# Attention's values in two matmuls a key tile instead of three, softmax sums on GpSimd, and three score banks for four

## The chip, the cores and the metric

The kernel runs on one core of one Trainium2 chip. The core has TensorE (PE, with its weight loads as PEld), VectorE (DVE), ScalarE (ACT), GpSimd (POOL) and SyncE (SP), which run their own instruction streams in order and wait for each other on semaphores. The metric is the device time of one execution in microseconds (µs), the median of three runs.

## The reference

One layer of a bidirectional hybrid encoder is applied to 2048 prompt tokens and 256 sample tokens (2304 together, 18 tiles of 128), in FP32:

```
n = rmsnorm(x);  p = n @ w_in            # 1024 -> 4*512 + 32 + 512 + 2*128
m = mlstm_mixer(...)                     # 8 heads, both directions, chunkwise
s = q . k * 64**-0.5;  P = softmax(s);  o = P @ v      # 8 query heads, 2 key/value heads, d = 64
x = x + concat(m, o) @ w_out
u = dwconv3(rmsnorm(x) @ w_up);  a, g = split(u);  y = rmsnorm(x + (silu(g) * a) @ w_down)
```

Attention is within a request: a prompt query sees the 16 prompt key tiles, a sample query the 2 sample key tiles. The scores are large (the norm weights of q and k carry a factor of 8), so that the softmax is taken with the row maximum subtracted.

## The kernel before

Matmuls run in FP32R, one pass a matmul. To keep FP32 precision an operand is split into a rounded high part and a low remainder, and a product is the sum of three matmuls (high·high, high·low, low·high) in one PSUM bank. The PSUM memory has eight banks; each holds 128 rows of 512 FP32 numbers.

The program has four stages. First the projections of attention's q, k, v and of the gates. Then attention and the mLSTM together: both are Python generators that emit their steps, and a planner (`run_both`) takes a step of the one that is behind, by costs that are written out (`A_PAIR`, `A_MAX`, `A_PREP` for attention, the numbers yielded by `mlstm`); a scheduler then reorders what was emitted by readiness and priority on each engine. After the mLSTM the output projection (`phase_c`, tile `po`) is emitted between attention's steps, and there PE keeps the order in which it was written. Last comes the feed-forward stage, more than half of the time, which the change does not touch.

Attention is worked in 36 blocks of 512 query columns, numbered 0 to 35 here in the order in which they run. Blocks 0, 1, 26 and 27 are the small ones (sample queries, 2 key tiles); the other 32 have 16 key tiles, worked in 8 pairs. Its steps in a large block:

- `prep`: four transposes of q (tile `pq`), copied by ACT.
- `maxstep`, 16 times: one matmul of 512 columns (tile `px`), then a row maximum on DVE (tile `mx`, L570). They are done one block ahead, while the scores of the block before run.
- `scores`, per key tile: two matmuls (L595, L596) into tile `ps`; ACT writes the exponential twice, rounded to `ph` (L599) and in FP32 back into `ps` (L600); DVE writes the remainder `pl = ps - ph` (L601).
- `values`, per key tile, two pairs behind the scores: three matmuls of 512 columns into the one bank `pv` (L613): [v high | ones] with `ph`, v low with `ph`, and [v high | ones] with `pl`. Rows 0 to 63 of `pv` gather the output, rows 64 to 127 the softmax sum, spread over 64 rows by the columns of ones.
- `fin1`: ACT copies both halves of `pv` out. `fin2`, four times: a reciprocal on DVE (L630). `fin3`: POOL multiplies (L634) and stores.

The tiles `pq`, `px`, `ps` and `pr` (the maxima, spread by a matmul) take turns in `SCB` = 4 banks of tag `sc`, one after the other in the order in which they are emitted; `pv` has one bank, and the mLSTM (or the output projection) has three.

The mLSTM works on four head pairs. For each there are the projections (PE, tiles `mj` and `mv`, 256 columns a matmul) and then 18 chunks of output, 72 in all, each with small FP32 matmuls (tiles `mS`, `mI`, `mN`, `mT`), some eight DVE operations on tiles `dm`, `s`, `dn` and `hh`, and on POOL a power (`mr`, L101), two selects on `dm` (L864) and the loads of `dm`.

Of the kernel before, what the change touches and what calls it, by code (L numbers as in the profile page):

```python
# [9 lines left out]
F32 = mybir.dt.float32  # L10
F32R = mybir.dt.float32r
AF = mybir.ActivationFunctionType
ALU = mybir.AluOpType
# [4 lines left out]
P = 128  # L18
# [6 lines left out]
HD = 64  # L25
# [4 lines left out]
ACOL = 2048  # L30
MPRI = 2000
STORE = "sync"
SCB = 4
MB = 2
MJ = 1
BLK = 768
# [21 lines left out]
DMB = 6  # L58
KWB = 2
LEAD = 1.3  # L60
A_PAIR = 2.3
A_MAX = 0.23
A_PREP = 1.0
C_MM = 1.43
# [10 lines left out]
PHB = 6  # L75
PLB = 6
# [12 lines left out]
def f32(ap):  # L89
    return ap.bitcast(F32)  # L90
# [382 lines left out]
def attention(g, tc, s1, s2, pp):  # L473


    nc = g.nc
    sp = s1
    hbs = []
    for grp in range(2):
# [4 lines left out]
        else:  # L484
# [2 lines left out]
                     for hh in (h0, h0 + 2)]  # L487
            hbs += large[0:8] + small + large[8:]
    kv = {}

    def load_kv(grp, k0, k1, after=None):

        if (grp, k0) in kv:
            return
        n = k1 - k0
        sp = s2 if n == NT1 else s1
        kv[(grp, k0)] = parts = []
        for t0 in range(0, n, 4):
            m = min(4, n - t0)
            s = f"{n}_{t0}"  # L500
            kk = sp.tile([P, m * P], F32R, tag="kk" + s, name=f"kk{grp}_{s}", bufs=1)
            kl1 = sp.tile([65, m * P], F32R, tag="kl1" + s, name=f"kl1{grp}_{s}", bufs=1)
            vs = [sp.tile([P, m, P if a == 0 else HD], F32R, tag=f"v{a}" + s, name=f"v{a}{grp}_{s}", bufs=1)
                  for a in range(2)]
            c = slice((k0 + t0) * P, (k0 + t0 + m) * P)
            if after is not None:
                for t in (kk[0:1, 0:1], kk[HD:HD + 1, 0:1], kl1[0:1, 0:1], vs[0][0:1, 0, 0:1], vs[1][0:1, 0, 0:1]):
                    nc.gpsimd.tensor_copy(t, after[0:1, 0:1])
            nc.gpsimd.memset(f32(vs[0][:, :, HD:]), 1.0)
            for r in (0, HD):  # L510
                nc.gpsimd.dma_start(f32(kk[r:r + HD, :]), g.k_d[grp, 0:HD, c])
            nc.gpsimd.dma_start(f32(kl1[0:HD, :]), g.k_d[grp, HD:P, c])
            nc.gpsimd.memset(f32(kl1[64:65, :]), 1.0)
            for a in range(2):
                nc.gpsimd.dma_start(f32(vs[a][:, :, 0:HD]), g.v_d[a, grp, :, k0 + t0:k0 + t0 + m])
            parts.append((kk, kl1, vs))

    class HB:
        pass
# [68 lines left out]
    def scores(s, kp):  # L588
        N = s.N
        parts = []  # L590
        for z in range(2):
            ps = pp.tile([P, 512], F32, tag="sc", name=f"ps{s.nm}_{kp}_{z}")[:, 0:N]
            kk, kl1, _ = s.kv[kp // 2]
# [6 lines left out]
            nc.scalar.activation(ps, ps, AF.Exp)  # L600
            nc.vector.tensor_tensor(pl, ps, f32(ph), ALU.subtract)  # L601
            parts.append((ph, pl))
        return parts

    def values(s, kp, parts):

        N = s.N
        if kp == 0:
            s.pv = pp.tile([P, 512], F32, tag="pv", name="pv" + s.nm, bufs=1)
        vs = [[v[:, (2 * kp + z) % 4, :] for v in s.kv[kp // 2][2]] for z in range(2)]  # L610
        todo = [(vs[z][k], parts[z][0]) for z in range(2) for k in range(2)] + [(vs[z][0], parts[z][1]) for z in range(2)]
        for k, (v, p) in enumerate(todo):
            nc.tensor.matmul(s.pv[0:HD if k in (1, 3) else P, 0:N], v, p, start=(kp == 0 and k == 0),  # L613
                             stop=(2 * kp + 2 == s.nk and k == 5))

    def fin1(s):

        N = s.N
        s.o1 = sp.tile([HD, 512], F32, tag="o1", name="o1" + s.nm, bufs=2)
        s.rs = sp.tile([HD, 512], F32, tag="rs", name="rs" + s.nm, bufs=1)  # L620
        nc.scalar.activation(s.o1[:, 0:N], s.pv[0:HD, 0:N], AF.Copy)
        nc.scalar.activation(s.rs[:, 0:N], s.pv[HD:P, 0:N], AF.Copy)
        s.left = list(range(0, N, P))

    def fin2(s):
# [958 lines left out]
```

## Time and profile before

| | µs |
|---|---|
| runs (3) | 3425.78, 3429.24, 3429.64; median 3429.24 |
| span of the profiled execution, first to last instruction | 3427.2 |
| PE / DVE / ACT / POOL busy | 3329.3 / 2677.3 / 1931.2 / 1120.9 |
| first and last score matmul of attention | 255.7 and 1756 |

The time of the profiled execution as a whole is not listed beside its span; the span lies between the three runs, 2.0 µs under their median, so that what lies around it is small against anything told here.

How to read it: a PE matmul's duration runs from its issue to its modelled end, and the next one starts long before that end; PE's busy share is therefore high even where it is not full, and what a matmul takes from PE is the step from its start to the start of the next. DMA issues, semaphores and register instructions are not counted as busy. "Idle before, releaser" names what ended an engine's wait.

### The profile page before, as it was taken

The numbers are of one execution on the slowest core, as the hardware profiler recorded it, in microseconds if no ns is written. First come the engines' busy times: TensorE is split into PE (matmuls) and PEld (weight loads), VectorE is DVE, ScalarE is ACT, GpSimd is POOL, SyncE is SP. The second block draws the span as 40 slices with busy tenths as digits, with TensorE's granted clock in tenths as the row PEclk, the third lists the DMA queues.
The fourth block names the chain that finished last, engine by engine and source line by source line (L and its number), as shares of the span: only waits on it lengthen the run. The fifth ranks groups of instructions, "written<-read, shape, count | busy, mean of one in ns | idle before, by whom it ended". The sixth has DMA issues, their size and how long they took to land. (4 is left out here: it accounts for less than half of the span.)

```text
span 3427.2 us, 55596 instructions
## 1 busy us (share of the span) xinstructions
PE 3329.3 (97%) x20058; PEld 3098.4 (90%) x20058; DVE 2677.3 (78%) x4654; ACT 1931.2 (56%) x4329; POOL 1120.9 (33%) x1328
## 2 busy tenths in 40 slices
PE   7989999999999999899999999999999999999998
PEld 6878888888888888688899999999999999999998
DVE  6885687777768788967767878789888888888776
ACT  4536666666666767655544444446444446555554
POOL 6653132213232323211244333226233224322222
PEclk9999999999999999999999999999999999999999
DMA  6765342333345444422365232223323213421221
GB/s 220 243 203 159 89 140 86 115 123 98 108 131 160 143 123 139 145 77 94 101 216 198 81 105 87 68 80 133 129 94 103 72 59 128 140 74 62 69 74 50
DMA packets 254756, 404.27 MB, mean 118 GB/s; under 512 B 32112, under 2 KB 156816, under 8 KB 254480
## 3 DMA queue, kind: packets, MB, share of 16 engines
q1 hardware_dynamic: 226576, 358.23, 32.7%
q0 software_dynamic: 11344, 33.04, 3.6%
q10 hardware_dynamic: 16560, 9.44, 0.9%
q8 instruction: 158, 2.59, 0.3%
q14 instruction: 118, 0.97, 0.1%
HBM read 316.73 MB, written 83.90 MB: 117 GB/s over the span
## 5 line engine op out<-in xcount | busy, mean ns | idle before, releaser
L1322 PE MATMUL pd<-act,wd 128*128 128x384 f32 (+1 forms) x3120 | 593.4, 336 | 23.9 <-DVE acc L1324 12.6
L1322 PEld LDWEIGHTS pd<-act,wd 128*128 128x128 f32 x3120 | 539.6, 188 | 32.6 <-DVE acc L1324 18.1
L601 DVE TENSOR_TENSOR pl<-ps,ph 128x512 fp32r<-128x512 f32 x520 | 352.7, 683 | 181.5 <-ACT ps L600 173.4
L1184 PE MATMUL pa<-nt,wut 128*128 128x386 f32 (+2 forms) x2376 | 454.3, 339 | 0.0
L599 ACT ACTIVATE ph<-ps 128x512 fp32r<-128x512 f32 x520 | 309.4, 595 | 243.5 <-PE ps L596 239.5
L1184 PEld LDWEIGHTS pa<-nt,wut 128*128 128x128 f32 x2376 | 421.6, 190 | 0.3 <-ACT u L1200 0.3
L570 DVE TENSOR_REDUCE mx<-px 128x1 f32<-128x512 f32 (+1 forms) x528 | 345.5, 670 | 74.4 <-PE px L569 72.4
L1278 DVE SCALAR_TENSOR_TENSOR y<-u,cw,y 128x768 f32<-128x768 f32 (+1 forms) x264 | 315.6, 1196 | 36.4 <-ACT y L1271 29.3
L1189 POOL TENSOR_TENSOR tw<-ru 128x512 f32<-128x512 f32 x66 | 94.1, 1425 | 732.5 <-DMA ru<-w_up 558.5
L613 PE MATMUL pv<-ph,v 128*128 128x512 f32 (+1 forms) x1040 | 319.4, 401 | 1.0 <-ACT ph L599 0.8
L600 ACT ACTIVATE ps<-ps 128x512 f32<-128x512 f32 x520 | 310.3, 597 | 0.0
L1200 ACT ACTIVATE u<-pa 128x386 f32<-128x386 f32 (+2 forms) x264 | 128.3, 486 | 320.9 <-PE pa L1184 320.7
L1324 DVE TENSOR_TENSOR acc<-pd,acc 128x384 f32<-128x384 f32 (+1 forms) x544 | 280.3, 535 | 35.5 <-PE pd L1322 34.1
L1041 PEld LDWEIGHTS po<-cmx,wo 128*128 128x128 f32 x1728 | 220.7, 191 | 8.2 <-DVE mmx L931 0.6
L1041 PE MATMUL po<-cmx,wo 128*128 128x256 f32 x1728 | 224.2, 284 | 0.4 <-DVE mmx L931 0.4
L595 PE MATMUL ps<-qq,kk 128*128 128x512 f32 x520 | 215.5, 416 | 4.2 <-DVE mx L570 2.4
L569 PE MATMUL px<-kk,qq 128*128 128x512 f32 (+1 forms) x528 | 202.8, 413 | 6.0 <-DVE mx L570 2.9
L596 PE MATMUL ps<-qm,kl 65*128 65x512 f32 x520 | 206.7, 399 | 0.0
L759 PE MATMUL mj<-mn,wm 128*128 128x256 f32 x1296 | 203.0, 289 | 2.8 <-ACT og L773 1.9
L759 PEld LDWEIGHTS mj<-mn,wm 128*128 128x128 f32 x1296 | 187.1, 193 | 19.8 <-ACT og L773 2.0
L769 PEld LDWEIGHTS mv<-wm,mn 128*128 128x128 f32 x1296 | 182.8, 190 | 18.4 <-ACT qb L765 2.5
L769 PE MATMUL mv<-wm,mn 128*128 128x256 f32 x1296 | 196.5, 285 | 1.0 <-ACT qb L765 0.9
(288 smaller groups left out, 7266.6 us busy)
## 6 DMA issues: line engine op xcount, KB each, us to landing
ru<-w_up SPq DMA_DIRECT2D x132, 512.0 KB, 3.4
mn<-n_d SPq DMA_DIRECT2D x216, 256.0 KB, 3.4
rd<-w_down SPq DMA_DIRECT2D x66, 512.0 KB, 3.6
n_d<-n1T SPq DMA_DIRECT2D x18, 1024.0 KB, 5.6
dm<-nm_d POOLq DMA_DIRECT2D x72, 256.0 KB, 4.1
mjn<-n_d SPq DMA_DIRECT2D x72, 256.0 KB, 3.3
mvn<-n_d SPq DMA_DIRECT2D x72, 256.0 KB, 3.1
q_d<-qz SPq DMA_DIRECT2D x18, 512.0 KB, 3.7
```

What stands on the lines that cost most here:

```text
L570: nc.vector.tensor_reduce(s.mx[:, t, z0:z0 + 1], ps[:, 0:w], AX.X, ALU.max)
L599: nc.scalar.activation(ph, ps, AF.Exp)
L600: nc.scalar.activation(ps, ps, AF.Exp)
L601: nc.vector.tensor_tensor(pl, ps, f32(ph), ALU.subtract)
L613: nc.tensor.matmul(s.pv[0:HD if k in (1, 3) else P, 0:N], v, p, start=(kp == 0 and k == 0), stop=(2 * kp + 2 == s.nk and k == 5))
L759: nc.tensor.matmul(pj[:, o], s.w[c][:, a, o * P:(o + 1) * P], nT[c][:, :, h, :], start=(c + o + k == 0), stop=(c == NCC - 1 and k == 2 and ...
L769: nc.tensor.matmul(pv[:, o], nT[c][:, o, a, :], s.w[c][:, h, 256:512], start=(c + o + k == 0), stop=(c == NCC - 1 and k == 2 and o == 1))
L1041: nc.tensor.matmul(po[:, o], wo[z // 2][c][:, a, n], mx[c][:, h, :], start=(c == 0 and k == 0), stop=(c == NCC - 1 and k == 2))
L1184: nc.tensor.matmul(p, w[:, aa, c, :], ops[k][:, c, bb, 0:n], start=c == 0 and i == 0 and not add, stop=c == NCC // 2 - 1 and i == 2, skip_ ...
L1278: nc.vector.scalar_tensor_tensor(y[:, s:e], u[:, s + k:e + k], cw[:, k, jj:jj + 1], y[:, s:e], ALU.mult, ALU.add)
L1322: nc.tensor.matmul(po, wds[j][c // 4][:, aa, c % 4 * P:(c % 4 + 1) * P], acts[j][:, bb, z0:z1], start=(j == 0 and k == 0), stop=(j == len( ...
L1324: nc.vector.tensor_tensor(accs[c][:, z0:z1], po, accs[c][:, z0:z1], ALU.add)
```

## The change

- **Two value matmuls.** The stationary operand of a key tile becomes one tile of 192 columns, [v low | v high | ones]. A matmul with columns 0 to 127 on `ph` writes `pv`: low·`ph` in rows 0 to 63, high·`ph` in rows 64 to 127. A matmul with columns 64 to 191 on `pl` writes a second bank, `pw`: high·`pl` and the sum of `pl`.
- **The sum of `ph`.** In blocks with 16 key tiles POOL adds the first 14 tiles `ph` into `pacc` (13 additions of 128x512), ACT rounds the total to a tile of tag `ph`, POOL writes its remainder to a tile of tag `pl`, and four matmuls with the constant tile `low` ([zeros | ones]) add the rounded total, the remainder and the last two `ph` to rows 64 to 127 of `pw`. Small blocks add their two `ph` by `low` directly.
- **`fin1`** copies rows 64 to 127 of `pv` to `o1` (ACT), adds rows 0 to 63 of `pv` and then of `pw` (two DVE operations of 64x512), and copies the sums out of `pw` (ACT). `o1` has one buffer instead of two.
- **Banks.** `SCB` goes from 4 to 3, and `pw` takes the bank.
- **The planner's cost** of a pair, `A_PAIR`, goes from 2.3 to 1.9.

```diff
-SCB = 4
+SCB = 3
+PSUMS = 14
-A_PAIR = 2.3
+A_PAIR = 1.9
...
+    low = s2.tile([P, P], F32R, name="low1")
+    nc.gpsimd.memset(f32(low[:, 0:HD]), 0.0)
+    nc.gpsimd.memset(f32(low[:, HD:P]), 1.0)
...
-            vs = [sp.tile([P, m, P if a == 0 else HD], F32R, tag=f"v{a}" + s, name=f"v{a}{grp}_{s}", bufs=1)
-                  for a in range(2)]
+            v = sp.tile([P, m, 3 * HD], F32R, tag="v" + s, name=f"v{grp}_{s}", bufs=1)
...
             parts.append((ph, pl))
+            i = 2 * kp + z
+            if s.nk > 2 and i < PSUMS:
+                if i == 1:
+                    s.acc = sp.tile([P, 512], F32, tag="pacc", name="pacc" + s.nm, bufs=1)[:, 0:N]
+                    nc.gpsimd.tensor_tensor(s.acc, f32(s.ph0), f32(ph), ALU.add)
+                elif i:
+                    nc.gpsimd.tensor_tensor(s.acc, s.acc, f32(ph), ALU.add)
+                else:
+                    s.ph0 = ph
+                if i == PSUMS - 1:
+                    s.tot = [sp.tile([P, 512], F32R, tag=t, name=f"{t}{s.nm}_s", bufs=n)[:, 0:N]
+                             for t, n in (("ph", PHB), ("pl", PLB))]
+                    nc.scalar.activation(s.tot[0], s.acc, AF.Copy)
+                    nc.gpsimd.tensor_tensor(s.tot[1], s.acc, f32(s.tot[0]), ALU.subtract)
...
-        todo = [(vs[z][k], parts[z][0]) for z in range(2) for k in range(2)] + [(vs[z][0], parts[z][1]) for z in range(2)]
-        for k, (v, p) in enumerate(todo):
-            nc.tensor.matmul(s.pv[0:HD if k in (1, 3) else P, 0:N], v, p, start=(kp == 0 and k == 0),
-                             stop=(2 * kp + 2 == s.nk and k == 5))
+        sums = list(s.tot) if last and s.nk > 2 else []
+        for z in range(2):
+            v = s.kv[kp // 2][2][:, (2 * kp + z) % 4]
+            ph, pl = parts[z]
+            nc.tensor.matmul(s.pv, v[:, 0:P], ph, start=kp + z == 0, stop=last and z == 1)
+            nc.tensor.matmul(s.pw, v[:, HD:], pl, start=kp + z == 0, stop=False)
+            if s.nk <= 2 or 2 * kp + z >= PSUMS:
+                sums.append(ph)
+        for i, p in enumerate(sums):
+            nc.tensor.matmul(s.pw, low, p, start=False, stop=last and i == len(sums) - 1)
...
-        nc.scalar.activation(s.o1[:, 0:N], s.pv[0:HD, 0:N], AF.Copy)
-        nc.scalar.activation(s.rs[:, 0:N], s.pv[HD:P, 0:N], AF.Copy)
+        nc.scalar.activation(o1, s.pv[HD:P], AF.Copy)
+        nc.vector.tensor_tensor(o1, s.pv[0:HD], o1, ALU.add)
+        nc.vector.tensor_tensor(o1, s.pw[0:HD], o1, ALU.add)
+        nc.scalar.activation(s.rs[:, 0:N], s.pw[HD:P], AF.Copy)
```

The banks and costs also move instructions that the diff does not name, since the scheduler places them anew. In the rows below the number that ends a name is an instruction's own number and means nothing; `ps_4_2_0` is the score tile of a block whose queries begin at tile 4, pair 2, first key tile of the pair.

PE, block 22, its third pair, before the change:

```order
L595 MATMUL ps_4_2_0_14623<-qq_4_13775,kk_16_4_11365 128x512
L596 MATMUL ps_4_2_0_14623<-qm_4_13777,kl_16_4_11366 128x512
L785 MATMUL mj_8_16348<-mjn_8_4_16336,wm_4_13569 128x256 x3
L595 MATMUL ps_4_2_1_14631<-qq_4_13775,kk_16_4_11365 128x512
L596 MATMUL ps_4_2_1_14631<-qm_4_13777,kl_16_4_11366 128x512
L613 MATMUL pv_4_14651<-pl_4_1_1_14596,v_16_0_11356 128x512
L889 MATMUL mI_15_15965<-C_15_9421,qb_7_9446 128x130 x2
L785 MATMUL mj_8_16348<-mjn_8_4_16336,wm_4_13569 128x256
L819 MATMUL mt_5_15982<-ident,mkT_5_13638 128x128 x2
L785 MATMUL mj_8_16348<-mjn_8_4_16336,wm_4_13569 128x256 x2
L785 MATMUL mj_8_16348<-mjn_8_5_16337,wm_5_13570 128x256 x3
L569 MATMUL px_4_0_2_14639<-kk_16_8_11376,qq_4_14411 128x512
```

The same place after the change (`ps_4_2_0` is now L598 and L599, `px` L572, `pv` L632, `pw` L633):

```order
L598 MATMUL ps_4_2_0_14807<-qq_4_13944,kk_16_4_11501 128x512
L599 MATMUL ps_4_2_0_14807<-qm_4_13946,kl_16_4_11502 128x512
L633 MATMUL pw_4_14838<-pl_4_1_1_14641,v_16_0_11493 128x512
L598 MATMUL ps_4_2_1_14816<-qq_4_13944,kk_16_4_11501 128x512
L599 MATMUL ps_4_2_1_14816<-qm_4_13946,kl_16_4_11502 128x512
L572 MATMUL px_4_0_2_14825<-kk_16_8_11511,qq_4_14589 128x512
L632 MATMUL pv_4_14837<-ph_4_2_0_14810,v_16_4_11503 128x512
L632 MATMUL pv_4_14837<-ph_4_2_1_14819,v_16_4_11503 128x512
L572 MATMUL px_4_1_2_14828<-kk_16_8_11511,qq_4_14589 128x512
L572 MATMUL px_4_2_2_14831<-kk_16_8_11511,qq_4_14589 128x512
L633 MATMUL pw_4_14838<-pl_4_2_0_14811,v_16_4_11503 128x512
L572 MATMUL px_4_3_2_14834<-kk_16_8_11511,qq_4_14589 128x512
```

The mLSTM's matmuls (`mj`, `mI`, `mt`) that stood between attention's are gone from here: they stand earlier. Over the whole program, 780 of the 3456 projection matmuls and 33 of the 72 output chunks stood behind block 19's first score, and now none does. Blocks 2 to 18 hold 39 chunks before and 72 after (16 of them in blocks 17 and 18, where there were 4), and blocks 19 to 27 hold attention alone.

POOL, around the power of chunk 14 of the first head pair, before the change:

```order
L856 DMA dm_2_9500<-nm_d 128x512
L864 AFFINE_SELECT dm_1_9453<-dm_1_9453 128x256 x2
L764 MEMSET qb_7_5300 64x2x128 x2
L100 TENSOR_SCALAR mr_14_8405<-mms_14_8402 128x2
L101 TENSOR_TENSOR mr_14_8405<-mr_14_8405,mhalf 128x2
L825 TENSOR_TENSOR kw_10_8434<-mkt_5_8432,tm 128x256
```

and after it (`dm` is loaded by L882 and selected by L890, L101 and L102 make the power):

```order
L612 TENSOR_TENSOR pacc_4_5122<-pacc_4_5122,ph_4_5_0_5528 128x512
L895 DMA ogr_0_9565<-og_d 128x256
L612 TENSOR_TENSOR pacc_4_5122<-pacc_4_5122,ph_4_5_1_5537 128x512
L612 TENSOR_TENSOR pacc_4_5122<-pacc_4_5122,ph_4_6_0_5721 128x512
L612 TENSOR_TENSOR pacc_4_5122<-pacc_4_5122,ph_4_6_1_5730 128x512
L882 DMA dm_2_9610<-nm_d 128x512
L890 AFFINE_SELECT dm_1_9557<-dm_1_9557 128x256 x2
L619 TENSOR_TENSOR pl_4_s<-pacc_4_5122,ph_4_s 128x512
L790 MEMSET qb_7_5327 64x2x128 x2
L101 TENSOR_SCALAR mr_14_8497<-mms_14_8494 128x2
L102 TENSOR_TENSOR mr_14_8497<-mr_14_8497,mhalf 128x2
L851 TENSOR_TENSOR kw_10_8526<-mkt_5_8524,tm 128x256
```

The mLSTM's steps on POOL now stand in one queue with the additions, each of which waits for ACT's `ph`.

15 lines of the change are left out of this document (8 added, 7 removed).

## The prediction

> **What bounds the kernel now.** I read the busy times by stretch first, cut at the first score matmuls of blocks 2, 19, 25, 29 and 35.
>
> ```profile
> span 3427.2 us, 55596 instructions
> 292.69 0.70 PE L595 MATMUL ps<-qq,kk 128*128 128x512 f32 x2
> 1063.81 0.39 PE L595 MATMUL ps<-qq,kk 128*128 128x512 f32 x1
> 1328.44 0.40 PE L595 MATMUL ps<-qq,kk 128*128 128x512 f32 x1
> 1450.93 0.39 PE L595 MATMUL ps<-qq,kk 128*128 128x512 f32 x1
> 1723.86 0.39 PE L595 MATMUL ps<-qq,kk 128*128 128x512 f32 x1
> core 0: us, PE busy (x) PEld busy (x) DVE busy (x) ACT busy (x) POOL busy (x), PEclk, DMA share, GB/s
> 292.70:1063.80 771.10, 767.52 (x4890) 675.98 (x4890) 568.16 (x1203) 516.59 (x1374) 192.75 (x391) 1.00 0.38 114
> 1063.80:1328.40 264.60, 263.42 (x1627) 225.73 (x1626) 214.78 (x499) 185.31 (x518) 83.11 (x170) 1.00 0.47 137
> 1328.40:1450.90 122.50, 112.25 (x664) 94.15 (x664) 107.15 (x259) 81.62 (x213) 32.48 (x62) 0.94 0.46 137
> 1450.90:1723.90 273.00, 267.37 (x1659) 232.93 (x1658) 196.34 (x344) 146.77 (x293) 44.98 (x47) 0.99 0.30 93
> 1400.00:1420.00 20.00, 15.52 (x71) 12.02 (x70) 18.79 (x54) 12.00 (x36) 5.25 (x11) 0.75 0.24 66
> ```
>
> PE is full from block 2 to block 24 (767.5 of 771.1, 263.4 of 264.6). DVE is second, at 568/771 = 74%, then 81%; in the mLSTM's tail, around 1400, DVE leads (18.8 of 20 µs) and PE waits. A timeline of one pair gives the steps, and what holds a score bank:
>
> ```profile
> 1502.69 0.40 PE L595 MATMUL ps<-qq,kk 128*128 128x512 f32 x1
> 1502.92 0.40 PE L596 MATMUL ps<-qm,kl 65*128 65x512 f32 x1
> 1503.15 0.40 PE L595 MATMUL ps<-qq,kk 128*128 128x512 f32 x1
> 1503.41 0.60 ACT L599 ACTIVATE ph<-ps 128x512 fp32r<-128x512 f32 x1 [2.31 <-PE ps L596]
> 1503.62 1.58 PE L1041 MATMUL po<-cmx,wo 128*128 128x256 f32 x12
> 1503.90 0.59 ACT L600 ACTIVATE ps<-ps 128x512 f32<-128x512 f32 x1
> 1504.42 0.59 ACT L599 ACTIVATE ph<-ps 128x512 fp32r<-128x512 f32 x1
> 1504.53 0.69 DVE L601 TENSOR_TENSOR pl<-ps,ph 128x512 fp32r<-128x512 f32 x1 [1.82 <-ACT ps L600]
> 1504.90 0.60 ACT L600 ACTIVATE ps<-ps 128x512 f32<-128x512 f32 x1
> 1505.24 0.69 DVE L1048 TENSOR_TENSOR cx<-po,cx 128x512 f32<-128x512 f32 x1
> ```
>
> A 512-column matmul takes 0.23 µs of PE (1502.69 to 1502.92); one of 256 columns about 0.118 (twelve in 1.58, the last with its tail of some 0.28). ACT starts one exponential every 0.5. A bank that takes scores at 1502.69 is free when `pl` ends at 1505.22, 2.53 µs later.
>
> **The change, part by part.** *Removed:* a large block had 48 value matmuls and has 32 + 4, so 12 x 0.23 = 2.76 µs of PE a block and 88.3 µs over 32 blocks. Small blocks keep 6. With PE full throughout, that would be the gain.
>
> *Added to POOL:* 14 operations of 128x512 a large block; to DVE two of 64x512 from PSUM, to ACT one copy.
>
> ```profile
> L1054 POOL TENSOR_TENSOR cacc<-cacc,csq x27: 1283/1292/2302, 1473.1 to 1832.1; 128x512 f32<-128x512 f32 x27
> L570 DVE TENSOR_REDUCE mx<-px 128x1 f32<-128x512 f32 (+1 forms) x426 | 278.9, 670 | 51.2 <-PE px L569 49.2
> L601 DVE TENSOR_TENSOR pl<-ps,ph 128x512 fp32r<-128x512 f32 x404 | 275.0, 684 | 130.1 <-ACT ps L600 126.9 <-PE pv L613 0.6 <-PE ps L596 0.3
> L630 DVE RECIPROCAL rs<-rs 64x128 f32<-64x128 f32 x112 | 95.4, 901 | 3.2 <-ACT rs L622 2.9
> 256.00:1440.00 1184.00, 1168.18 (x7370) 1018.96 (x7368) 904.95 (x1988) 792.93 (x2128) 336.77 (x684) 0.99 0.42 124
> ```
>
> POOL: 14 x 1.29 = 18.1 µs a block, 578 in all, in a queue that had 337 µs of work over 1184. DVE: the nearest row for an addition from PSUM is L1048's 0.69, as long as any 512-column DVE row here; two are 1.4 µs a block. A block's DVE work becomes 16 x 0.67 + 16 x 0.684 + 4 x 0.90 + 1.4 + 0.3 (the small `mx` rows) = 27.0. ACT: 0.6, hidden.
>
> *Moved* (the order on PE): all of the mLSTM's matmuls now stand ahead of block 19. So there are now three stretches, and I sum them instead of claiming the 88.
>
> Blocks 19 to 27 have **attention alone** on PE: 84 matmuls, 19.3 µs, and 0.7 of small ones, 20.0 a large block. Nothing fills PE's waits there, so latency decides. Half of a block's pairs carry two scores and four maxima through three banks. Scores at 0 and 0.46 free their banks at 2.5 and about 3.5 (ACT reaches the second 1.0 later); the second and third maximum need those two banks, their reductions queue behind that `pl` and end near 4.2 and 4.9, and the next pair's scores take their places. A pair lasts 4.2, with 4 x 0.67 + 2 x 0.684 = 4.05 µs of DVE in it: 17 for four. The last block's reciprocals and additions (3.6 + 1.4) find little room on DVE: +3.5. The four pairs without maxima go at ACT's pace, four exponentials at 0.5, with little lost: 8.5. The boundary (transposes, ACT's copies, and the last values, which wait for POOL's remainder while the next block's maxima and values queue behind them on PE) I put at 2.5. Together 31.5; the lower bound is DVE's own 27.0, the upper 36, with nothing overlapped at the boundary. Block 25, whose successor has 4 maxima only, 24; block 26, 10; block 27, with 16 maxima for block 28, 15; block 28, 32. So 6 x 31.5 + 24 + 10 + 15 + 32 = **270**, where blocks 19 to 28 took 1450.9 - 1063.8 = 387.1: **-117**.
>
> **Mixed**, blocks 2 to 18. At their steps the matmuls there now make 732 of the 771.1 µs (95%). Now 17 x 2.76 = 47 go, and 780 projections at 0.118 (92) and 33 chunks at 1.7 (56) come: 833. DVE: the 905 of 256 to 1440 less attention's 279 + 275 + 95 leave 256 for 72 chunks, 3.55 each. In blocks 2 to 11 (36 chunks) PE has 523 and DVE 398: PE's, at 0.94, 556. In blocks 12 to 18 (36 chunks) PE has 310, DVE 7 x 27.0 + 36 x 3.55 = 317: neither hides the other. At the 0.94 that DVE reached around 1400, 317 gives 337, if nothing makes DVE's operations longer; something does:
>
> ```profile
> L910 DVE TENSOR_TENSOR hh<-s x72: 217/282/1114, 450.4 to 1435.6; 128x128 f32<-128x128 f32 x72
> L919 DVE TENSOR_TENSOR hh<-hh,mr x72: 270/293/1134, 453.3 to 1439.1; 128x128 f32<-128x128 f32 x72
> L921 DVE SCALAR_TENSOR_TENSOR hh<-ogr,hh x54: 217/292/1602, 454.4 to 1255.1; 128x128 f32<-128x128 f32 x54
> L601 DVE TENSOR_TENSOR pl<-ps,ph x520: 617/683/694, 260.8 to 1762.0; 128x512 fp32r<-128x512 f32 x174
> ```
>
> DVE operations with both inputs in SBUF have medians of 0.28 to 0.29 and maxima of 1.1 to 1.6, while `pl`, with one input in PSUM, never passes 0.694; and a POOL addition of median 1.29 has a maximum of 2.30. In this trace the long ones overlap a POOL operation. With additions on 18.1 of about 52 µs, 35%, such an operation waits 0.35 x 0.65 = 0.23 on average; six a chunk (three on `hh`, one on `s`, two on `C`) make 36 x 6 x 0.23 = 50 µs: (317 + 50)/0.94 = 390. Between 337 and 390 I take 355, nearer the lower end, since what waits is mostly not at the end of a chain. Mixed: 556 + 355 = **911**, against 771: **+140**. The bounds are 833/0.95 = 877 and 570 + 400 = 970.
>
> The SBUF — State Buffer page of the Trainium skill (section "SBUF: two separate sides") calls the port pair of VectorE and GpSimd an exclusive lock, held for the whole instruction, which a VectorE operation with two SBUF inputs takes against a GpSimd operation that reads SBUF. The rows above agree; by the rule alone each meeting costs up to a full addition, 1.29 µs, and the sum would sit at the upper end.
>
> **With the output projection**, blocks 29 to 34: 273/6 = 45.5 a block, PE's steps 42.7 of it. 2.76 go; but where no `po` stands between scores and maxima, the second maximum now waits for a `pl`:
>
> ```profile
> PEld ps L595 <- DVE mx L570: 5.0, 8, 1.5
> PEld px L569 <- DVE pl L601: 3.6, 6, 1.6
> ```
>
> PE's loads already wait so between 1400 and 1770, with four banks, up to 1.6 µs; one or two such waits more a block, 2.2 µs, eat most of the gain. **-3** (bounds -17 and +6), and -1.5 for the last block. What follows has PE's old work.
>
> Sum: 3427.2 - 117 + 140 - 3 - 1.5 = 3445.7, rounded to **3445** (+0.5%). Two µs between span and median change nothing.
>
> **Rivals.** *Fewer banks do not bind* (the other side, faster): attention alone runs at DVE's own 27.0, the mixed stretch keeps 95%. Then 6 x 27 + 20 + 8 + 13 + 27 = 230 (-157), 877 (+106), -3 and -1.5: 3372. For it speaks DVE's 94% around 1400; against it, that the mLSTM's operations gave DVE work there while a bank was held. It decides if an alone block stays below 29 µs.
>
> *POOL and its port lead* (slower still). In blocks 12 to 18 the upper 390 holds (+35), and POOL falls behind: by count, its own work between the multiplications of blocks 16 and 17 is 55 µs, 17 of it additions, in a block that I give about 51. The powers then come late, with `hh` and PE's `mT` behind them: +15 more, 3495. Against it: with few additions in the queue
>
> ```profile
> POOL mr L100 <- ACT s L913: 268.0, 58, 17.0
> ```
>
> POOL waits for ACT, 268 µs in all, so there is room. It decides from a backlog that outlasts a block.
>
> *PE stays full*: -88.3, 3339. The order speaks against it: 20.0 µs of PE work cannot fill a block that needs 27.0 of DVE.
>
> **How the numbers follow.** My forecast 0.50, POOL and port 0.23, banks do not bind 0.20, full gain 0.07. A measurement here tells about 0.2% (7 µs) from no change. The last two are faster, 0.27 less a little for their slower edge; of my case, whose own range is 3415 to 3475, 0.12 falls within 0.2%, 0.02 below, the rest slower. Faster 0.26, same 0.12, slower 0.62. The range that leaves out 2 in 10 is 3360 to 3510: it takes in the case that banks do not bind, with a little room below, and most of POOL's; about 0.11 is left below, most of it the full gain, and 0.08 above.
>
> **What would show it.** Block 19's first scores near 1204 (292.7 + 911); from there to block 25 PE's busy share falls clearly under 90% and first scores lie about 31.5 µs apart, with PE waiting for `mx` and `pl`; blocks 29 to 34 stay near 45 µs; two-input DVE rows on `hh` and `C` have higher means between 300 and 1200. It is wrong if alone blocks take 28 µs or less, or if block 19 starts before 1175 or after 1235.

## The result and the profile after

The changed kernel takes **3625.17 µs** (median of 4 runs, 3619.13 to 3632.97) against 3428.76 for the kernel before on the same chip (4 runs, 3425.78 to 3429.64): a ratio of **1.0577, 95% interval 1.0561 to 1.0594**. It is 196 µs slower; 3445 had been forecast. The profiled execution has a span of 3617.4 µs, 190.2 more than the 3427.2 before.

First the span and the first score matmuls of blocks 2, 19, 25, 29 and 35 from the timeline of PE (start, duration, engine, line, tile), as they stand in the prediction for the kernel before.

```profile
span 3617.4 us, 55861 instructions
295.17 0.46 PE L598 MATMUL ps<-qq,kk 128*128 128x512 f32 x1
1292.41 0.80 PE L598 MATMUL ps<-qq,kk 128*128 128x512 f32 x1
1508.17 0.50 PE L598 MATMUL ps<-qq,kk 128*128 128x512 f32 x1 [0.86 <-ACT qm L562]
1603.39 0.47 PE L598 MATMUL ps<-qq,kk 128*128 128x512 f32 x1
1913.76 0.48 PE L598 MATMUL ps<-qq,kk 128*128 128x512 f32 x1
```

And the busy times between them, in the same four stretches as before (mixed, attention alone up to block 24, blocks 25 to 28, blocks 29 to 34 with the output projection):

```profile
core 0: us, PE busy (x) PEld busy (x) DVE busy (x) ACT busy (x) POOL busy (x), PEclk, DMA share, GB/s
295.20:1292.40 997.20, 944.31 (x6047) 835.52 (x6045) 795.00 (x1656) 626.66 (x1789) 592.11 (x830) 0.97 0.43 133
1292.40:1508.20 215.80, 174.85 (x553) 105.14 (x552) 162.38 (x260) 125.76 (x247) 122.04 (x103) 0.87 0.13 37
1508.20:1603.40 95.20, 74.09 (x261) 49.09 (x261) 66.81 (x110) 51.09 (x97) 46.62 (x41) 0.80 0.06 17
1603.40:1913.80 310.40, 268.05 (x1575) 229.98 (x1574) 202.39 (x338) 148.09 (x289) 152.91 (x131) 0.95 0.23 73
```

| stretch | before | after | difference | forecast |
|---|---|---|---|---|
| up to block 2 | 292.7 | 295.2 | +2.5 | 0 |
| mixed, blocks 2 to 18 | 771.1 | 997.2 | **+226** | +140 |
| blocks 19 to 28 | 387.1 | 311.0 | **-76** | -117 |
| blocks 29 to 34 | 273.0 | 310.4 | **+37** | -3 |
| block 35 and all behind it | 1703.3 | 1703.6 | 0 | -1.5 |

PE is nowhere full any more: 95% of the mixed stretch, 81% and 78% alone, 86% with the output projection. The column behind POOL's is the TensorE clock that was granted. It falls to 0.87, 0.80 and 0.95 in the last three stretches, where the kernel before had 1.00, 0.94 and 0.99.

A second reading divides the time of blocks 2 to 34 into two parts. Each matmul has a step, the distance from its start to the next start. The **PE steps** are the sum of the steps that its kind (output tile and shape) has when matmuls stand back to back, taken as the median of the shorter 60% of that kind's steps in all runs together; **what lies between** is the rest: waits, gaps and lengthening by a lower clock. The kernel before has 1313 + 118 µs, the changed one 1225 + 394. So the change did take 88 µs of steps off PE, as counted, and put 276 µs of lost time in between. The experiments ask where the 276 come from.

Two candidates lead. **Theory 1:** the bank that the scores lost. **Theory 2:** the additions on GpSimd, by their queue or by the port that they share with VectorE. The rows of VectorE speak for the second. Ahead, three groups of operations with two SBUF inputs, and `pl`, of the kernel before (instructions | busy, mean ns | idle before, releaser):

```profile
L849 DVE SCALAR_TENSOR_TENSOR C<-C,dec,C 128x65 f32<-128x65 f32 x128 | 37.9, 300 | 16.0 <-ACT C L841 14.0
L907 DVE TENSOR_TENSOR s<-s,dn 128x256 f32<-128x256 f32 x72 | 30.9, 429 | 1.2
L921 DVE SCALAR_TENSOR_TENSOR hh<-ogr,hh 128x128 f32<-128x128 f32 x54 | 21.9, 406 | 0.5
L601 DVE TENSOR_TENSOR pl<-ps,ph 128x512 fp32r<-128x512 f32 x520 | 352.7, 683 | 181.5 <-ACT ps L600 173.4 <-PE po L1041 4.8 <-PE pv L613 0.6
```

and the same four in the changed kernel, with its additions:

```profile
L875 DVE SCALAR_TENSOR_TENSOR C<-C,dec,C 128x65 f32<-128x65 f32 x128 | 55.5, 437 | 15.0 <-ACT C L867 13.4
L933 DVE TENSOR_TENSOR s<-s,dn 128x256 f32<-128x256 f32 x72 | 41.2, 573 | 1.5
L947 DVE SCALAR_TENSOR_TENSOR hh<-ogr,hh 128x128 f32<-128x128 f32 x54 | 33.0, 612 | 0.8
L604 DVE TENSOR_TENSOR pl<-ps,ph 128x512 fp32r<-128x512 f32 x520 | 352.7, 682 | 196.7 <-ACT ps L603 193.8
L612 POOL TENSOR_TENSOR pacc<-pacc,ph 128x512 f32<-128x512 f32 x384 | 498.8, 1299 | 309.0 <-ACT ph L602 295.2
```

The mean of an operation with both inputs in SBUF has grown by 0.14 to 0.21 µs; `pl`, which takes one input from PSUM, has not moved. If it is the port, it does not show as a wait here (the idle time before `C` is 16.0 and 15.0 µs) but as a longer operation.

For the first theory speak PE's waits in blocks 29 to 34, where no mLSTM is left (who waited <- for whom: µs in all, times, longest). Before:

```profile
PE px L569 <- DVE pl L601: 1.1, 1, 1.1
PE px L569 <- DVE mx L570: 1.0, 3, 0.5
```

After:

```profile
PE px L572 <- DVE mx L573: 34.2, 25, 3.6
PE px L572 <- DVE pl L604: 5.1, 9, 1.3
```

The maxima wait for a bank that an earlier maximum or score still holds: 39 µs instead of 2.

### The profile page after: what moved, and what is told of

Same layout as the page of the kernel before. It is cut to its first block, busy times and chain, and to the rows that moved or that the text cites. A ratio compares the mean times of both kernels' runs of the same rounds, so it can differ in the third digit from the quotient of the medians.

```text
span 3617.4 us, 55861 instructions
## 1 busy us (share of the span) xinstructions
PE 3382.5 (94%) x19674; PEld 3091.5 (85%) x19674; DVE 2824.5 (78%) x4726; ACT 1955.1 (54%) x4361; POOL 1691.0 (47%) x1778
## 4 chain that ended last, share of the span: by engine, by line
PE 61%; DVE 19%; ACT 6%; DMA 5%; issue 5%; POOL 3%; SPq 0%; ACTq 0%; DVEq 0%; POOLq 0%
PE pa L1210 12%; PE pd L1348 11%; PE pc L1210 6%; PE po L1067 4%; PE mv L795 4%; PE mj L785 3%; PE px L572 3%; PE pb L1210 2%; PE pv L632 2%; PE pw L633 2%; PE ps L598 2%; DVE mx L573 2%; PE ps L599 2%; DVE pl L604 2%; DVE rs L656 2%
## 5 line engine op out<-in xcount | busy, mean ns | idle before, releaser
L612 POOL TENSOR_TENSOR pacc<-pacc,ph 128x512 f32<-128x512 f32 x384 | 498.8, 1299 | 309.0 <-ACT ph L602 295.2
L1304 DVE SCALAR_TENSOR_TENSOR y<-u,cw,y 128x768 f32<-128x768 f32 (+1 forms) x264 | 314.5, 1192 | 36.2 <-ACT y L1297 29.1
L572 PE MATMUL px<-kk,qq 128*128 128x512 f32 (+1 forms) x528 | 236.6, 470 | 79.4 <-DVE mx L573 60.8
L598 PE MATMUL ps<-qq,kk 128*128 128x512 f32 x520 | 232.5, 447 | 30.3 <-DVE mx L573 14.2
L632 PE MATMUL pv<-ph,v 128*128 128x512 f32 x520 | 224.0, 441 | 24.4 <-ACT ph L602 23.1
L572 PEld LDWEIGHTS px<-kk,qq 128*128 128x128 f32 x528 | 107.1, 204 | 143.7 <-DVE mx L573 91.2
L633 PE MATMUL pw<-pl,v 128*128 128x512 f32 x520 | 216.7, 423 | 2.3 <-ACT rs L648 1.7
L599 PE MATMUL ps<-qm,kl 65*128 65x512 f32 x520 | 215.7, 415 | 0.0
L785 PE MATMUL mj<-mn,wm 128*128 128x256 f32 x1296 | 194.2, 289 | 4.8 <-ACT og L799 3.6
```

The source lines that it names most:

```text
L572: nc.tensor.matmul(ps[:, 0:w], s.qq[:, t * P:(t + 1) * P], s.kv[z0][0][:, 0:w], start=True, stop=True)
L598: nc.tensor.matmul(ps, kk[:, kc:kc + P], s.qq[:, 0:N], start=True, stop=False)
L612: nc.gpsimd.tensor_tensor(s.acc, s.acc, f32(ph), ALU.add)
L785: nc.tensor.matmul(pj[:, o], s.w[c][:, a, o * P:(o + 1) * P], nT[c][:, :, h, :], start=(c + o + k == 0), stop=(c == NCC - 1 and k == 2 and ...
L1304: nc.vector.scalar_tensor_tensor(y[:, s:e], u[:, s + k:e + k], cw[:, k, jj:jj + 1], y[:, s:e], ALU.mult, ALU.add)
```

## The experiments

All times are medians; ratios stand against the kernel before on the same chip. The table gives all runs first; the value matmuls are those of a large block, the sums' included, and the last two columns are the two parts of blocks 2 to 34.

| run | score banks | value matmuls | GpSimd | µs | ratio, 95% interval | PE steps | between |
|---|---|---|---|---|---|---|---|
| before | 4 | 48 | - | 3428 | 1 | 1313 | 118 |
| e1_banks3 | 3 | 48 | - | 3556 | 1.0365 (1.0350 to 1.0381) | 1308 | 239 |
| e6_before_sums | 4 | 48 | additions | 3508 | 1.0235 (1.0219 to 1.0250) | 1314 | 196 |
| e7_memsets | 4 | 48 | fills | 3444 | 1.0048 (1.0032 to 1.0064) | 1314 | 129 |
| e8_v1_no_sums | 4 | 34 | - | 3395 | 0.9903 (0.9890 to 0.9917) | 1213 | 182 |
| v1_one_bank | 4 | 36 | additions | 3510 | 1.0237 (1.0221 to 1.0252) | 1227 | 281 |
| e2_no_sums | 3 | 34 | - | 3513 | 1.0242 (1.0225 to 1.0259) | 1211 | 307 |
| e11_after_memsets | 3 | 36 | fills | 3531 | 1.0301 (1.0276 to 1.0325) | 1225 | 304 |
| the change | 3 | 36 | additions | 3625 | 1.0577 (1.0561 to 1.0594) | 1225 | 394 |
| e3_apair | 3 | 36 | additions | 3632 | 1.0602 (1.0588 to 1.0617) | 1228 | 397 |
| e5_sums_pe | 3 | 48 | - | 3588 | 1.0464 (1.0449 to 1.0478) | 1311 | 262 |
| v2_hybrid | 4 | 48; 36 in six blocks | additions in six | 3441 | 1.0039 (1.0025 to 1.0052) | 1296 | 140 |
| v3_hybrid | 4 | 48; 36 in six blocks | additions in six | 3433 | 1.0008 (0.9997 to 1.0019) | 1297 | 143 |

### One bank fewer, and nothing else

The edit is to the kernel before.

```diff
-SCB = 4
+SCB = 3
```

> The kernel before with SCB = 3 and nothing else (one PSUM bank stays unused); 48 value matmuls a block, no additions on GpSimd. Theory 1, the lost score bank makes the loss (its waits, the earlier mLSTM that it makes the scheduler choose, and PE's lower clock behind both): 3500 to 3570 us, with attention-alone blocks 33 to 36 us apart, blocks 29 to 34 above 49 us, and clock windows of 0.5. Theory 2, the additions on GpSimd make it (queue and port): 3425 to 3460 us, blocks 29 to 34 at 45 to 46 us.

Measured: 3556, +128 µs, as the first theory has it in sum, and more than the second allows. Blocks 29 to 34 take 312.8 µs (273 before, 310.4 after the change), so **the whole loss of that stage is the bank's**. Its waits there:

```profile
PE px L569 <- DVE mx L570: 20.8, 21, 3.4
PE px L569 <- DVE pl L601: 13.3, 9, 2.9
```

The bank alone also makes the scheduler bring the mLSTM forward: 184 of 3456 projections and 10 of 72 chunks stand behind block 19, where it was 780 and 33. The smaller value step packs too: with four banks, the runs with 36 and with 34 value matmuls below have 240 and 499 projections there. One expectation missed. The blocks that have attention alone are 30.4 µs apart, not 33 to 36, though PE has 12 more matmuls in them than in the change:

```profile
1349.37 0.39 PE L595 MATMUL ps<-qq,kk 128*128 128x512 f32 x1
1379.95 0.39 PE L595 MATMUL ps<-qq,kk 128*128 128x512 f32 x1
1410.32 0.39 PE L595 MATMUL ps<-qq,kk 128*128 128x512 f32 x1
1440.68 0.39 PE L595 MATMUL ps<-qq,kk 128*128 128x512 f32 x1
```

### The additions, and nothing else

The kernel before, with the additions in `scores` and a total that nobody uses. To make room, `o1` has one buffer, as in the change.

```diff
+            if s.nk > 2 and i < PSUMS:
+                    nc.gpsimd.tensor_tensor(s.acc, s.acc, f32(ph), ALU.add)
...
+                    nc.scalar.activation(s.tot[0], s.acc, AF.Copy)
+                    nc.gpsimd.tensor_tensor(s.tot[1], s.acc, f32(s.tot[0]), ALU.subtract)
```

> The kernel before, four score banks and three value matmuls, plus the 13 additions, ACT's rounding and the remainder of the softmax sum in each large block, whose result nobody uses (o1 has one buffer for room). Theory 1 (banks): 3430 to 3465 us; PE hides the longer two-input operations of DVE, which gain 60 to 100 us in sum. Theory 2 (additions): 3530 us or more, with blocks 12 to 18 over 55 us apart.

Measured: 3508, +80 µs, between the two theories' ranges. Blocks 29 to 34 are untouched (272.6 µs, with all the additions in them); the 80 µs lie in blocks 2 to 28 (1237.5 for 1158.2), where the mLSTM runs. Neither theory alone holds: the bank costs 128, the additions 80, and their sum of 208 is already more than the change's loss of 196.

### The change without its additions

The edit is to the changed kernel.

```diff
-                    nc.gpsimd.tensor_tensor(s.acc, s.acc, f32(ph), ALU.add)
...
-        sums = list(s.tot) if last and s.nk > 2 else []
+        sums = []
```

> The changed kernel without the additions: no pacc, no rounding and remainder, and only the last two ph by the constant tile, so that the softmax sum leaves out 14 of 16 key tiles; 34 value matmuls a block, three banks. Theory 1 (banks): 3540 to 3610 us, blocks 29 to 34 still above 49 us, alone blocks 32 to 35 us. Theory 2 (additions): 3400 to 3450 us.

Measured: 3513, 112 µs under the change and 85 over the kernel before; again between the ranges. Blocks 29 to 34 keep their loss (307.1 µs).

### All parts with four banks

The edit is to the changed kernel.

```diff
-SCB = 3
+SCB = 4
-            nc.tensor.matmul(s.pw, v[:, HD:], pl, start=kp + z == 0, stop=False)
+            nc.tensor.matmul(s.pv[0:HD], v[:, HD:P], pl, start=False, stop=False)
...
+            s.pw = pp.tile([P, 512], F32, tag="sc", name="pw" + s.nm)[:, 0:N]
+            nc.tensor.matmul(s.pw[0:HD], low[:, HD:P], p, start=i == 0, stop=i == len(s.sums) - 1)
```

> Both are kept: 36 value matmuls a block and all additions on GpSimd, but with SCB = 4. The product v high by pl accumulates in rows 0 to 63 of pv, and the sum's four matmuls (a column tile of ones, 64 rows out) use a bank of tag sc at the block's end; the sum of pl, below 0.1% of the softmax sum, is left out of it; one addition of 64x512 fewer on DVE. Theory 1 (banks): 3360 to 3420 us, faster than before. Theory 2 (additions): 3520 us or more. If both needed each other to do harm, about 3470 us.

Measured: 3510, 115 µs under the change, but not under the kernel before; the first theory's 3360 to 3420 fails, and so, by 10 µs, does the second's 3520 or more. Blocks 29 to 34 fall to 261.6, 11 µs under the kernel before: this is what two matmuls are worth where PE is full and no mLSTM is there (of 6 x 2.76 = 17 µs counted). Blocks 2 to 28 stay at 1246.4, 88 over.

Against the run with unused sums, which has the same additions and score banks, PE's steps fell by 87 µs and what lies between rose by 85. In that company PE's work had no price at all.

### Queue or port

The edit is to the run with unused sums.

```diff
-                    nc.gpsimd.tensor_tensor(s.acc, s.acc, f32(ph), ALU.add)
+                nc.gpsimd.tensor_copy(s.acc[0:1, 0:1], f32(ph)[0:1, 0:1])
+                nc.gpsimd.memset(s.acc, 0.0)
+                nc.gpsimd.memset(s.acc, 0.0)
```

> The kernel before with four banks and three value matmuls; where the run with unused sums had an addition on GpSimd, GpSimd now copies one number of ph (which keeps the wait for ACT) and then fills the 128x512 tile twice with zeros, which reads no SBUF. GpSimd's queue is as full and waits as often, but VectorE's operations meet no long GpSimd operation that reads. If the port makes the +80 us of that run: 3425 to 3450 us, with DVE's two-input rows back near 0.29 us. If the queue makes it (the mLSTM's GpSimd steps come late): 3490 to 3515 us.

Measured: 3444, +16 µs where the additions cost 80. GpSimd is as busy as with them: 0.527 + 0.526 + 0.180 = 1.23 µs for each key tile against 1.30.

```profile
L609 POOL MEMSET pacc<- 128x512 f32 x448 | 235.9, 527 | 24.2
L610 POOL MEMSET pacc<- 128x512 f32 x448 | 235.9, 526 | 22.3
L608 POOL COPY pacc<-ph 1x1 f32<-1x1 f32 x448 | 80.9, 180 | 342.6 <-ACT ph L600 328.6 <-POOL pacc L610 0.3
L857 DVE SCALAR_TENSOR_TENSOR C<-C,dec,C 128x65 f32<-128x65 f32 x128 | 38.9, 308 | 13.7 <-ACT C L849 11.8
```

VectorE's `C` is back at 0.308 (0.300 before), while in the run with unused sums it had nearly doubled:

```profile
L864 DVE SCALAR_TENSOR_TENSOR C<-C,dec,C 128x65 f32<-128x65 f32 x128 | 74.6, 585 | 12.8 <-ACT C L856 11.2
```

So the queue costs some 16 µs at most, `o1`'s single buffer included, and the exchange gains 64. Not all of the 64 need be the reading of SBUF by GpSimd: the exchange also leaves out ACT's rounding of the total, for which ACT waited 17.1 µs in all in the run with unused sums (14 times, up to 2.6). If all of that counted, 47 would be left for the reading. The Trainium skill states why reading matters on the page "SBUF — State Buffer", section "SBUF: two separate sides": a VectorE operation with two SBUF inputs locks against GpSimd only where GpSimd's operation reads SBUF. The two runs agree with it, 0.308 against fills and 0.585 against additions.

The same exchange was made in the change itself, since PE's order differs there.

```diff
-                    nc.gpsimd.tensor_tensor(s.acc, s.acc, f32(ph), ALU.add)
+                nc.gpsimd.tensor_copy(s.acc[0:1, 0:1], f32(ph)[0:1, 0:1])
+                nc.gpsimd.memset(s.acc, 0.0)
+                nc.gpsimd.memset(s.acc, 0.0)
...
-                sums.append(ph)
+                sums += [ph] * (2 if s.nk > 2 else 1)
```

> The changed kernel with GpSimd's additions replaced as in the run with zeros: one number of ph copied, then the 128x512 tile filled twice, so that GpSimd is as busy and waits as often, and reads next to nothing. ACT's rounding is left out, and in place of the rounded total and the remainder the last two ph are added twice, so the softmax sum leaves out 14 of 16 key tiles and PE keeps its 36 value matmuls. PE's order is packed as in the change (no projection and one chunk behind block 19's first score). If the port makes what the additions cost (112 us between the change and the run of it without additions): 3515 to 3550 us, VectorE's two-input rows at their old means. If the queue or the packed order makes it: 3590 to 3625 us.

Measured: 3531, 94 µs under the change and 18 over the run without additions: the port again, with the packed order kept, and with the total's rounding on ACT left out again. The mixed stretch shrinks from 997 to 919 µs (first scores of blocks 2 and 19 at 294.6 and 1213.5), and the blocks that have attention alone from 34.2 to 32.0, here blocks 22 to 24:

```profile
1318.90:1415.10 96.20, 81.90 (x278) 49.04 (x278) 75.88 (x121) 58.59 (x114) 58.70 (x136) 0.93 0.05 14
```

ACT's wait for the total, which goes with the rounding, is 13.9 µs in the change, far from the 94:

```profile
ACT ph_s L618 <- POOL pacc L612: 13.9, 12, 2.0
```

`C` is at its old mean, and ACT's waits for `hh`, 17.9 µs in the kernel before and 70.7 in the change, are down to 29.1. The group of `C` in this run:

```profile
L868 DVE SCALAR_TENSOR_TENSOR C<-C,dec,C 128x65 f32<-128x65 f32 x128 | 36.9, 291 | 9.2 <-ACT C L860 7.4
```

Its wait, and then that of the changed kernel:

```profile
ACT s L932 <- DVE hh L929: 29.1, 23, 5.1
```

```profile
ACT s L939 <- DVE hh L936: 70.7, 37, 5.9
```

The operations on `hh`, `s`, `C` and `dn` lengthened by 84 µs in all in the change (the difference of the means by the count of each group), about as much as the exchange gains. In the run with unused sums they lengthened by 118, and there the exchange gains only 64. So no fixed share of the lengthening reaches the time. VectorE is 80% busy in the mixed stretch of the change, so it would have had 200 µs of idle time to take them in. That they cost so much there all the same may be because they stand one behind the other in a chunk, with ACT's `s` and PE behind them; that this chain is why, and not a queueing of attention's `pl` and `mx` behind it, the runs do not show.

### What two matmuls a key tile are worth by themselves

The edit is to the run with all parts and four banks.

```diff
-                    nc.gpsimd.tensor_tensor(s.acc, s.acc, f32(ph), ALU.add)
...
-            s.sums = list(s.tot) + s.sums
...
-        nc.scalar.activation(s.rs[:, 0:N], s.pw[0:HD], AF.Copy)
+        nc.scalar.activation(s.rs[:, 0:N], s.pw[0:HD], AF.Copy, bias=1.0)
```

> Four score banks, one value bank, 32 value matmuls and two for the sum a block, nothing on GpSimd: the run with all parts and four banks without its additions. The softmax sum leaves out 14 of 16 key tiles, the sum of pl is left out too, and a constant of 1 is added to keep it positive. It prices 14 fewer matmuls alone. If PE sets the time: 14 x 0.23 x 32 = 103 us less than before, about 3330 us. If what PE gives up comes back as PE waits, as 84 of 87 us did between the two runs with additions and four banks: 3415 to 3430 us. I expect 3380 to 3410, some of both.

Measured: 3395, -33 µs of 103 counted. The run keeps the change's other parts (a pair's cost of 1.9, `o1`'s single buffer, one addition on VectorE a block, and for the sum a turn in the score banks at the block's end), so this is the worth of the matmuls with them. PE's steps fell by 100, what lies between rose by 64. Blocks 29 to 34 gave 23 µs; blocks 2 to 28 gave 12 (1145.9 for 1158.2), although 79 µs of steps went there. The reason shows in the rows of blocks 24 to 28:

```profile
1314.00:1438.50 124.50, 100.11 (x352) 64.45 (x350) 96.32 (x170) 75.17 (x150) 12.83 (x17) 0.81 0.20 60
1438.50:1687.90 249.40, 244.68 (x1563) 211.97 (x1561) 187.46 (x332) 142.62 (x283) 44.81 (x47) 1.00 0.28 90
```

The mLSTM's projections are used up in block 23 and its last chunk ends early in block 24, and then PE starves at 80% busy and a clock of 0.81. PE work that is saved in the mixed stretch comes back as attention alone, whose blocks are bounded by latency. With the sums left out it is no kernel to use; it shows what this code would gain if they cost nothing.

### More matmuls again

The changed kernel without additions on GpSimd, and with one more matmul for each key tile.

```diff
+            nc.tensor.matmul(s.pw, low, ph, start=False, stop=last and z == 1)
```

> The changed kernel with all sums on PE: each ph by the constant tile right behind its values, 48 value matmuls a block, no additions on GpSimd, three banks, two value banks. Against the run of the change without additions (34 matmuls, 3513 us) it has 14 x 0.23 x 32 = 103 us more of PE work. If PE's work counts there: 3590 to 3615 us. If the matmuls only fill PE's waits and keep its clock up, as the 30.4 us alone blocks of the run with three banks and 48 matmuls suggest: 3535 to 3560 us, alone blocks 30 to 32 us apart at a granted clock near 1.00.

Measured: 3588, 75 µs over the run without additions, of 103 counted. My expectation, that they would fill waits, fails: only about a quarter of them did. Its alone blocks lie 33.1 µs apart, not 30.4, at a clock of 0.95; so the number of matmuls does not explain the short blocks of the run with three banks. What differs is seen at a block's end, here in the changed kernel (start, duration, line; in brackets the wait):

```profile
1381.56 3.37 DVE L656 RECIPROCAL rs<-rs 64x128 f32<-64x128 f32 x4
...
1382.26 0.40 PE L572 MATMUL px<-kk,qq 128*128 128x512 f32 x1
1384.85 0.62 DVE L573 TENSOR_REDUCE mx<-px 128x1 f32<-128x512 f32 x1
...
1385.53 0.50 PE L572 MATMUL px<-kk,qq 128*128 128x512 f32 x1 [2.87 <-DVE mx L573]
```

The four reciprocals of the block before run in one piece of 3.37 µs, the maxima queue behind them on VectorE, and with three banks PE has nowhere to write: a hole of 3.27 µs between two starts. In the run with sums on PE the holes are 3.17 µs in each block, in the one without additions 3.50; in the run with three banks and the old value step the reciprocals are as long, but PE finds values to multiply and its longest hole is 1.18. The third bank alone is not the reason: the run with all parts and four banks has holes of 3.17 there too, where its sum takes a turn in the score banks, and its blocks are 31 to 32 µs apart.

The clock follows. Rows of the change (blocks 20 to 24) and of the run with three banks alone (blocks 22 to 24):

```profile
1335.80:1508.20 172.40, 142.00 (x461) 85.77 (x461) 127.51 (x203) 100.78 (x194) 101.63 (x85) 0.91 0.05 14
```

```profile
1349.40:1440.70 91.30, 83.30 (x314) 49.52 (x313) 71.65 (x116) 58.30 (x113) 7.12 (x9) 1.00 0.06 15
```

The page "TensorE: Matmul & The Clock Gate" of the Trainium skill, section "Part 1: The HAM clock gate (the "warmup" mystery)", has the clock halved after an idle window of about 3.4 µs. The traces agree in the sign, 1.00 where holes stay under 1.2 µs; they differ in the length, since in blocks 22 to 24 of the change the longest hole is 2.61 µs and the clock still falls. Nor does the longest hole decide alone: in block 25 of the run with unused sums it is 2.26 µs, and the clock stays at 1.00. While half the clock is granted, a 512-column matmul's step is 0.43 µs in the change, not 0.23. An estimate of the price, counting at most a doubling of the step of each matmul that started then: 68 µs in blocks 2 to 34 of the change, 7 in the kernel before, 49 in the change with fills. Waits that fell into this time are in it, and no run separates it.

### The planner's cost of a pair

The edit is to the changed kernel.

```diff
-A_PAIR = 1.9
+A_PAIR = 2.3
```

> The changed kernel with A_PAIR back at 2.3, nothing else. PE's order in blocks 0 to 28 does not move, so blocks 2 to 28 keep 1308 us; only the pace of the output projection between attention's steps in blocks 29 to 35 changes. If the planner's cost is no cause: 3615 to 3635 us. If it makes the loss in the stage with the output projection (37 us there): 3585 to 3595 us.

Measured: 3632. It is no cause: blocks 29 to 34 gain 3 µs (306.9), and what is lost lies in blocks 2 to 28 (1318 for 1308), where PE's order is the same up to the middle of block 28, and from block 35 on (1711 for 1704).

### Two matmuls only where they paid

The kernel before, with the value step of the run with four banks in blocks 29 to 34 only.

```diff
+A_PAIR2 = 1.95
+TWO = range(29, 35)
...
+        s.two = n in TWO
...
+        if not s.two:
+            todo = [(vs[z][:, HD:] if k == 0 else vs[z][:, 0:HD], parts[z][0]) for z in range(2) for k in range(2)]
...
+            nc.tensor.matmul(s.pv, vs[z][:, 0:P], ph, start=kp + z == 0, stop=end)
```

> Four banks; the kernel before's three matmuls in blocks 0 to 28 and 35, and in blocks 29 to 34, where the output projection fills PE and no mLSTM is left on DVE, two value matmuls with the additions on GpSimd and one value bank (the sum of pl, below 0.1%, is left out of the softmax sum there). The run with all parts and four banks had these six blocks in 261.6 us where the kernel before has 272.9, and lost 10 us behind them, where the last block's additions stood ahead of the output projection's own sums on GpSimd. If the stage decides: 3412 to 3421 us, 0.2 to 0.5% faster than before. If o1's single buffer or the order costs something: 3425 to 3440 us.

Measured: 3441, +13 µs. Blocks 29 to 34 took 252.1, but some 11 µs of that is output projection that the planner had moved ahead of them (PE steps of 231 where the run with four banks has 241), and block 28, with the mLSTM's last chunks, took 67.7 for 43.8. The next run puts back what had changed outside the six blocks.

```diff
-A_PAIR2 = 1.95
+A_PAIR2 = 2.3
-O1B = 1
+O1B = 2
...
-                    s.acc = sp.tile([P, 512], F32, tag="pacc", name="pacc" + s.nm, bufs=1)[:, 0:N]
+                    s.acc = sp.tile([P, 512], F32, tag="o1", name="pacc" + s.nm, bufs=O1B)[:, 0:N]
```

> As the version with two value matmuls in blocks 29 to 34 alone, with three things put back that it had changed outside them: o1 has two buffers again (pacc takes turns with o1 in them), the constant tile is gone (the ones of the value tile serve), and a pair costs the planner 2.3 everywhere. The sum of pl is still left out of the softmax sum in these six blocks. That version had these blocks in 252 us for 273, and lost 26 us in blocks 2 to 28 (most of it in block 28, with the mLSTM's last chunks) and 5 behind the last block. If o1's single buffer or the planner's costs made that loss: 3405 to 3418 us. If two matmuls in a late stage always move the mLSTM's tail: 3430 to 3445 us.

Measured: 3433, a ratio of 1.0008 (0.9997 to 1.0019): no difference. Block 28 is back at 40.5, but blocks 29 to 34 now take 272.2: PE's steps fell by 17 µs there, and the time between rose by 16, in waits of scores and maxima for `mx` and `pl`. So the gain of 11 µs in the run with four banks is not reproduced by nearly the same code in another neighbourhood (here `pacc` takes turns with `o1`, and a pair costs 2.3), and no version was found that beats the kernel before.

## Why the prediction was wrong

The direction was right (slower, 0.62) and the size was not: 3625 against 3445 and an upper end of 3510. By its steps:

**Removed work and order: right.** 88 µs of PE work counted, 88 found. The mixed stretch was to gain 101 µs of steps (833 for 732) and gained 94. The mLSTM stands ahead of block 19 as the order said.

**The port in the mixed stretch, "Between 337 and 390 I take 355, nearer the lower end, since what waits is mostly not at the end of a chain": this is the step that failed most.** Of the 172 µs between forecast and profile, 86 lie in this stretch (997 for 911). I let 18 µs of the lengthening count, in blocks 12 to 18, and none in blocks 2 to 11, where PE was to hide it. The exchange of additions for fills, with PE's order packed as in the change, makes the stretch 78 µs shorter (919), with the total's rounding on ACT as the other thing that it leaves out. Blocks 12 to 18 took 422 µs for 355, with fills 379; blocks 2 to 11 took 575 for 556, with fills 540 (there the change has some 120 projections and two chunks more). Block 17, with the last chunks, took 86 µs for 49.

That the price of the port looks well sized is luck: 0.23 µs for six operations in each of 72 chunks are 99 µs, and 84 were measured, but the six I named (three on `hh`, one on `s`, two on `C`) make only 54 of them, 0.14 µs each, and two small operations on `dn`, which I had not listed, the other 30. So the step that failed is how much of the lengthening reaches the time; that most of it does so in the change is shown, by which chain stays open.

**The bank in the mixed stretch: the smaller part there.** I let the lost bank act there through the order and a share of 0.94 alone. By itself it costs 77 µs in blocks 2 to 28 (1234.9 for 1158.2). But with fills, with three banks and the packed order, the mixed stretch takes 919 µs, where the forecast without its 18 for the port has 893: 26 µs for bank and queue together.

**"With the output projection ... one or two such waits more a block, 2.2 µs ... -3 (bounds -17 and +6)": mechanism right in the main, size wrong.** Waits of maxima and scores for a bank did come, though mostly for `mx` (34 µs of PE's waits) and little for `pl` (5), which I had put first. With 16.6 µs of work gone and 37 lost, they and what follows from them cost 54 µs in six blocks, 9 a block, four times the 2.2. I had priced them by the longest wait that four banks left (1.6 µs) and one or two of them a block; with three banks they come one behind another, up to 3.6 µs, and the bound of +6 had no such case.

**Attention alone: 31.5 µs a block forecast, 34.2 found; -117 forecast, -76 found.** The reciprocals, 3.5 µs with no room on VectorE, are in the trace (3.37 in one piece). With fills these blocks are 32.0 µs apart at a granted clock of 0.93, near the forecast, so most of the 2.7 µs a block comes with the additions or ACT's rounding, by what wait the runs do not show. The rest of the 41 µs is block 19 (43.4 µs, still with the mLSTM's end) and blocks 25 to 28 (95 for 81). That the clock falls, to 0.87 in blocks 19 to 24, was not in the forecast; its share is not shown.

**The rivals.** "POOL and its port lead" (3495) had the port right and the other half wrong: a full queue costs 16 to 18 µs, and VectorE waits for the power `mr` for 23.3 µs in all, 2.0 at most, where it waited 28.3 before, so GpSimd does not fall behind. It also needed the bank's waits with the output projection, which stood in no case. "Fewer banks do not bind" falls with the first run: +128. "PE stays full" falls with the run that has four banks and no additions: 33 of 103 µs.

**What was to show it.** Block 19's first scores at 1292, above the 1235 at which I called the forecast wrong; alone blocks under 90% busy with waits for `mx` and `pl`, as said; blocks 29 to 34 at 52 µs, not 45; two-input rows longer, as said.

The pieces nearly add up. By the table, a bank costs 113 to 125 µs of lost time wherever it is taken (118 to 239, 182 to 307, 281 to 394), the additions 78 to 99 (118 to 196, 307 to 394, 182 to 281), and fewer matmuls give 87 to 100 of steps and bring 64 to 85 of lost time. For the change: -88 of steps, +64 to +85 of waits that the freed PE time turns into, +120 or so for the bank and +80 to +100 for the additions: +176 to +217, and +187 was measured in blocks 2 to 34. The lower clock is inside these pieces, not beside them.

## What to carry to other kernels

Price a freed instruction only where its engine is full after the change too: of 100 µs of PE work taken off a kernel that kept PE 97% busy, 33 µs reached the time. A PSUM bank that double-buffers a chain through several engines can be worth more than the matmuls that it pays for; count how many producers of different length take turns in it. And work that is "put on an idle engine" is not free when it is GpSimd that reads SBUF beside VectorE operations with two SBUF inputs: count the latter, and do not take VectorE's idle time as room for them.

## What the runs showed of the hardware that was not expected

- GpSimd operations that only write SBUF leave VectorE alone: with fills of 0.527 µs filling GpSimd's queue, `C` takes 0.291 to 0.308 µs, with additions of 1.30 µs 0.437 to 0.585.
- Where attention runs alone, the granted clock falls to 0.89 to 0.93 while PE is 82 to 86% busy by the profile's count, with one hole of 2.4 to 3.5 µs in a block of 31 to 35 µs, and stays at 1.00 with holes of 1.2 and PE 91% busy. One block with the mLSTM's end, PE at 82% and a hole of 2.26 µs kept 1.00, so no threshold follows. Taking matmuls out can so make the others slower; how much of the change's loss this is stays an estimate.
